# The later adaLN modulations of a two-layer mixer: vector times matrix by TensorE, or elementwise by VectorE with one-column products

## The chip, the cores and the metric

One core of one Trainium2 chip runs the whole program. The metric is the device time of one execution in microseconds; a kernel's time is the median over its runs.

## What is computed

Two layers over 1024 latent and 256 context tokens of width 1024. Each layer takes a modulated layer norm, one wide input projection, four token mixers, a gated merge of their outputs and an output projection. What the change touches is the modulation: for each of two conditions (`c` for the latent tokens, `c_ctx` for the context) a vector of 1024 numbers times a 1024 x 3072 matrix, plus a bias.

```python
def modulation(cond, w_mod, b_mod):
    mod = jax.nn.silu(cond) @ w_mod + b_mod
    return jnp.split(mod, 3, axis=-1)
...
    shift, scale, gate = modulation(c[:, None, :], w_mod, b_mod)
    p_lat = (layer_norm(x) * (1.0 + scale) + shift) @ w_in
    acc = sum(jax.nn.sigmoid(ms[i]) * ((ys[i] * jax.nn.silu(zs[i])) @ w_branch[i]) for i in range(N_BRANCH))
    x_new = layer_norm(DEEPNORM_ALPHA * x + gate * out) * ln_g + ln_b
```

## The kernel before

Most products take float32 operands split into a high and a low part (`hi_lo`, `split_w`), and each is done as three TensorE products (L299 to L301 and L307 to L309). The engines are TensorE (PE; its weight loads, the stationary operand, are listed as PEld), VectorE (DVE), ScalarE (ACT), GpSimd (POOL) and SyncE (SP), which issues most DMAs. The program is written as Python generators; `weave` takes steps from two of them in turn. A scheduler then sets a fixed order of the instructions on each engine, and each engine and each DMA queue works through its order without overtaking.

**The merge stage** (`merge`, L981 to L1004) follows the attention of each layer. For each of the four branches, in the order 2, 3, 1, 0, it loads the branch's output from DRAM (`load_u`: six loads `merge__tmp<-start__u`, L973, each split into `uh` and `ul` by ACT at L312 and DVE at L313). Then for each of eight column blocks `c` and each token group (256, 512 and 512 tokens in layer 0; 512 and 512 in layer 1) it makes a gate and a branch product. For even `c` the gate is computed there: 24 TensorE products into `merge__mm` (two PSUM buffers). For odd `c` the gate was computed during the attention and is loaded from DRAM (`merge__tmp<-start__gates`, L992). ACT takes the sigmoid (L996) into a `tmp` tile (three buffers). Six TensorE products into one of three banks of the PSUM tile `wide` give the branch product. DVE multiplies the two (L1000 for the first branch, L1002 after it) and adds (L1003, on POOL for odd `c`). Weights arrive as `merge__wraw` and are split by ACT (L263) and DVE (L264).

**The later modulations.** `modulation` for the first 2048 columns of layer 0 runs at the program's start. The others (`later_mods`: 1024 gate columns of layer 0, 2048 shift and scale columns of layer 1, 1024 gate columns of layer 1) are a generator that is woven into the merge stage of layer 0 as `mod0`. It loads 64 tiles of 128 rows x 512 columns of `w_mod` (`mod__wm`, tag `q`, three buffers, L185). The two condition vectors (`sc`, 128 x 2 for each of eight row blocks `k`) are the stationary operand, and 256 or 512 columns of weights stream past (L188): 96 float32 products into rows 0 and 1 of four column groups of one PSUM bank (tag `pv`, a single buffer). The result lies in rows, so ACT copies it out (L194, 12 copies), TensorE transposes it in 32 pieces of 128 columns (L197), and DVE adds the bias (L199). `last__gate` (L1014) then writes a gate to DRAM in 4-byte elements, and it is read back as rows in the output projection.

Of the kernel before, what the change touches and what calls it, by code (L numbers as in the profile page):

```python
# [8 lines left out]
F32 = mybir.dt.float32  # L9
F32R = mybir.dt.float32r  # L10
AF = mybir.ActivationFunctionType
ALU = mybir.AluOpType
# [5 lines left out]
KC = D // 128  # L18
# [29 lines left out]
def hybrid_kernel(ctx: ExitStack, tc, a):  # L48
    nc = tc.nc
    pe, act, dve, pool, sp = nc.tensor, nc.scalar, nc.vector, nc.gpsimd, nc.sync  # L50
# [3 lines left out]
    tp = ctx.enter_context(tc.tile_pool(name="tp", bufs=2))  # L54
    sm = ctx.enter_context(tc.tile_pool(name="sm", bufs=4))
    lc = ctx.enter_context(tc.tile_pool(name="lc", bufs=2))
# [19 lines left out]
    def nm(s):  # L76
        ids[0] += 1
        return f"{phase[0]}__{s}_{ids[0]}"
# [4 lines left out]
    def weave(*streams):  # L83

        live = [[0, n, label, gen] for label, gen, n in streams]
        while live:
            s = min(live, key=lambda s: (s[0] + 0.5) / s[1])
            phase[0] = s[2]
            s[0] += 1
            if next(s[3], live) is live:  # L90
                live.remove(s)
# [81 lines left out]
    def modulation(l, base, ncols, out, stage, sw):  # L173

        acc = ps_v.tile([128, 512], F32, tag="pv", name=nm("pm"))
        g = 4
        w_ = ncols // g
        n = ncols // 128
        bm = lc.tile([128, 16], F32, tag="bm", name=nm("bm"))
        sp.dma_start(bm[:, :n], a["b_mod"][l, :, base // 128:base // 128 + n])  # L180
        for k in range(KC):
            for h in range(ncols // sw):
                w = stage()
                c0 = base + h * sw
                sp.dma_start(w, a["w_mod"][l, k * 128:(k + 1) * 128, c0:c0 + sw])  # L185
                for j in range(sw // w_):
                    q = 32 * (h * sw // w_ + j)
                    pe.matmul(acc[q:q + 2, :w_], sc[:, k, :], w[:, j * w_:(j + 1) * w_],  # L188
                              start=k == 0, stop=k == KC - 1)
                yield  # L190
        tps = tbank()
        for j in range(g):
            row = tmp()
            act.copy(row[0:2, :w_], acc[32 * j:32 * j + 2, :w_])  # L194
            for i in range(w_ // 128):
                c = j * (w_ // 128) + i
                pe.transpose(tps[:, 2 * c:2 * c + 2], row[0:2, i * 128:(i + 1) * 128], ident[0:2, 0:2])  # L197
        mc = lc.tile([128, 2, 16], F32, tag="modc", name=nm("modc"), bufs=4)
        dve.tensor_tensor(mc[:, :, :n].rearrange("p s n -> p n s"),  # L199
                          tps[:, :2 * n].rearrange("p (n s) -> p n s", s=2),  # L200
                          bm[:, :n, None].to_broadcast([128, n, 2]), ALU.add)
        if n == 16:
            dve.tensor_scalar(mc[:, :, 8:16], mc[:, :, 8:16], 1.0, None, ALU.add)
        out["m"] = mc
        yield
# [109 lines left out]
    def layer(l, xh, xl, need_ctx, gate, finish, side, ahead=None):  # L315
# [663 lines left out]
        def merge():  # L979
            for bi, i in enumerate(M_ORDER):  # L980
                uh, ul = load_u(i, bi % 2 == 0)  # L981
                for c in range(KC):
                    w = None if (i, c) in gate_d else load_chunk(a["w_chunks"][l, GATE_0 + i * KC + c])
                    wb = load_chunk(a["w_branch"][l, i, c])
                    if bi == 0:
                        acc[c] = slot(s="acc")
                    for g in qgroups:
                        gs = slice(g[0], g[0] + g[1])
                        sgm = tmp()
                        if w is None:  # L990
                            pm = sgm
                            sp.dma_start(sgm[:, :g[1]], gate_d[i, c][:, gs])  # L992
                        else:
                            pm = mm()
                            mm_b(pm[:, :g[1]], w, xs_g(g))
                        act.activation(sgm[:, :g[1]], pm[:, :g[1]], AF.Sigmoid)  # L996
                        pb = sbank()
                        mm_b(pb[:, :g[1]], wb, lambda k: (uh[k][:, gs], ul[k][:, gs]))
                        if bi == 0:
                            dve.tensor_mul(acc[c][:, gs], pb[:, :g[1]], sgm[:, :g[1]])  # L1000
                        else:
                            dve.tensor_mul(sgm[:, :g[1]], pb[:, :g[1]], sgm[:, :g[1]])  # L1002
                            (pool if w is None else dve).tensor_add(acc[c][:, gs], acc[c][:, gs], sgm[:, :g[1]])  # L1003
                        yield  # L1004

        for _ in fill["gen"]:
            pass
        weave((f"merge{l}", merge(), 4 * KC * len(qgroups)), (f"mod{l}", side, 68))


        phase[0] = f"last{l}"
# [143 lines left out]
    ctx.push(pools)  # L1155
    x1 = dr.tile([SEQ, D], F32, name="x1", bufs=1)

    def raw_w():
        return tp.tile([128, 512], F32, tag="q", name=nm("wm"), bufs=3)

    def later_mods():
        yield from modulation(0, 2048, 1024, gate0, raw_w, 512)
        yield from modulation(1, 0, 2048, mc1, raw_w, 512)
        yield from modulation(1, 2048, 1024, gate1, raw_w, 512)

    def fin0(t, Y, later):
        if t >= CT:
# [99 lines left out]
```

## Time and profile before

| | |
|---|---|
| median of 3 runs | 2960.34 us (2957.03 to 2962.0) |
| the profiled execution | 2960.92 us, span 2959.1 us |
| busy in the span | PE 94%, DVE 51%, ACT 41%, POOL 14% |
| mean granted TensorE clock | 0.977 of full speed |
| chain of work that ended last | PE 75%, DVE 7%, DMA 4%, ACT 4% |

A busy share is an average over stages. A matmul's listed duration contains its latency; what it costs in a stream is the distance from its start to the start of the next. "Releaser" is the instruction that ended an engine's wait. For a DMA, the time "to landing" runs from its issue to the arrival of its data.

### The profile page before, as it was taken

What the parts mean: (1) busy time and instruction counts of PE and PEld (TensorE: products, weight loads), DVE (VectorE), ACT (ScalarE), POOL (GpSimd) and SP (SyncE); (2) the same over time, 40 slices, a digit from 0 to 9 for tenths busy, and PEclk for the clock granted to TensorE, in tenths of its full rate; (3) what the DMA queues carried; (4) which work ended last, traced back from release to release, by engine and by line L of the source; (5) the groups of instructions that cost most, each with busy time, mean ns of one, the idle gap of its engine ahead of it and who ended that gap; (6) DMA issues with size and microseconds to landing.
All of it is one profiled execution on the core that took longest, in us unless ns stands there. A gap on an engine that the chain in (4) does not pass through costs nothing.

```text
span 2959.1 us, 40218 instructions
## 1 busy us (share of the span) xinstructions
PE 2790.4 (94%) x14458; PEld 2253.0 (76%) x14458; DVE 1508.0 (51%) x3069; ACT 1219.0 (41%) x2631; POOL 418.8 (14%) x507
## 2 busy tenths in 40 slices
PE   7997979999999999899999798999999999999998
PEld 3785858888888887677767576778888888777776
DVE  5644266555555552232458554356555556533456
ACT  4344256445455542222234434346545455522230
POOL 1210020110111100111222120012111111001131
PEclk9998989999999999999999898999999999999999
DMA  6333322222223333333332333423222323222232
GB/s 248 115 107 102 107 72 84 84 84 87 88 88 123 103 98 111 104 120 104 124 98 90 91 103 111 117 74 102 80 93 78 106 103 126 87 94 87 86 109 91
DMA packets 240424, 301.83 MB, mean 102 GB/s; under 512 B 27488, under 2 KB 160096, under 8 KB 240224
## 3 DMA queue, kind: packets, MB, share of 16 engines
q1 hardware_dynamic: 134368, 225.58, 24.2%
q10 hardware_dynamic: 105856, 73.68, 8.0%
q8 instruction: 114, 1.87, 0.3%
q14 instruction: 86, 0.70, 0.1%
HBM read 217.11 MB, written 82.07 MB: 101 GB/s over the span
## 4 chain that ended last, share of the span: by engine, by line
PE 75%; DVE 7%; DMA 4%; ACT 4%; issue 2%; POOL 2%; ACTq 1%; SPq 0%; DVEq 0%; POOLq 0%
PE wide L639 6%; PE merge__mm L307 4%; PE merge__mm L308 4%; PE merge__mm L309 4%; PE wide L307 3%; PE wide L308 3%; PE wide L309 3%; PE m_att__t L584 3%; PE g_att__t L584 2%; PE a_att__mm L307 2%; PE a_att__mm L308 2%; PE a_att__mm L309 2%; PE m_att__mm L309 2%; PE m_att__mm L308 2%; PE m_att__mm L307 2%
## 5 line engine op out<-in xcount | busy, mean ns | idle before, releaser
L307 PE MATMUL merge__mm<-xh,merge__whi 128*128 128x512 f32 (+1 forms) x640 | 243.0, 380 | 0.9 <-ACT a_att__tmp L934 0.9
L308 PE MATMUL merge__mm<-xl,merge__whi 128*128 128x512 f32 (+1 forms) x640 | 239.6, 374 | 0.0
L309 PE MATMUL merge__mm<-xh,merge__wlo 128*128 128x512 f32 (+1 forms) x640 | 239.4, 374 | 0.0
L313 DVE TENSOR_TENSOR m_att__pl<-m_att__t,m_att__ph 128x384 fp32r<-128x384 f32 (+1 forms) x248 | 122.1, 508 | 117.2 <-ACT m_att__ph L312 78.8
L263 ACT CAST merge__whi<-merge__wraw 128x256 fp32r<-128x256 f32 (+1 forms) x128 | 65.6, 513 | 255.6 <-PE merge__mm L308 176.7
L1002 DVE TENSOR_TENSOR merge__tmp<-wide,merge__tmp 128x512 f32<-128x512 f32 (+1 forms) x120 | 76.5, 637 | 184.8 <-PE wide L309 161.2
L1003 POOL TENSOR_TENSOR merge__acc<-merge__acc,merge__tmp 128x512 f32<-128x512 f32 (+1 forms) x60 | 79.2, 1320 | 585.9 <-DVE merge__tmp L1002 585.8
L307 PEld LDWEIGHTS merge__mm<-xh,merge__whi 128*128 128x128 f32 x640 | 120.6, 188 | 44.5 <-issue 19.9
L312 ACT CAST m_att__ph<-m_att__t 128x384 fp32r<-128x384 f32 (+1 forms) x248 | 105.0, 439 | 115.3 <-PE m_att__t L584 103.5
L313 DVE TENSOR_TENSOR g_att__pl<-g_att__t,g_att__ph 128x384 fp32r<-128x384 f32 (+1 forms) x228 | 111.3, 514 | 79.6 <-ACT g_att__ph L312 58.4
L307 PE MATMUL wide<-merge__uh,merge__whi 128*128 128x256 f32 (+1 forms) x320 | 127.4, 398 | 20.4 <-ACT merge__uh L312 11.5
L264 DVE TENSOR_TENSOR merge__wlo<-merge__wraw,merge__whi 128x256 fp32r<-128x256 f32 (+1 forms) x128 | 71.0, 555 | 141.2 <-ACT merge__whi L263 134.3
L309 PEld LDWEIGHTS merge__mm<-xh,merge__wlo 128*128 128x128 f32 x640 | 120.8, 189 | 23.9 <-issue 0.4
L308 PEld LDWEIGHTS merge__mm<-xl,merge__whi 128*128 128x128 f32 x640 | 120.8, 189 | 22.3
L312 ACT CAST g_att__ph<-g_att__t 128x384 fp32r<-128x384 f32 (+1 forms) x228 | 97.7, 446 | 69.3 <-PE g_att__t L584 65.3
L307 PE MATMUL a_att__mm<-xh,a_att__whi 128*128 128x512 f32 (+1 forms) x320 | 123.8, 387 | 0.0
L641 DVE TENSOR_SCALAR_CACHE_REDUCE m_att__p<-wide 128x1280 f32<-128x1280 f32 (+1 forms) x72 | 98.7, 1371 | 42.1 <-PE wide L639 41.8
L309 PE MATMUL a_att__mm<-xh,a_att__wlo 128*128 128x512 f32 (+1 forms) x320 | 120.1, 377 | 0.0
L639 PE MATMUL wide<-g_att__ks,g_att__q 128*128 128x512 f32 (+1 forms) x400 | 103.5, 365 | 17.5 <-DVE g_att__p L641 16.3
L308 PE MATMUL a_att__mm<-xl,a_att__whi 128*128 128x512 f32 (+1 forms) x320 | 120.0, 375 | 0.0
L299 PE MATMUL a_proj__mm<-a_proj__whi,xh 128*128 128x256 f32 (+1 forms) x320 | 112.0, 351 | 8.1 <-ACT a_proj__tmp L809 4.5
L308 PE MATMUL wide<-merge__ul,merge__whi 128*128 128x256 f32 (+1 forms) x320 | 119.6, 374 | 0.0
(418 smaller groups left out, 7919.4 us busy)
## 6 DMA issues: line engine op xcount, KB each, us to landing
merge__wraw<-in_w_chunks_dram SPq DMA_DIRECT2D x64, 256.0 KB, 2.9
mod__wm<-in_w_mod_dram SPq DMA_DIRECT2D x64, 256.0 KB, 3.0
g_proj__wm<-in_w_mod_dram SPq DMA_DIRECT2D x16, 512.0 KB, 9.8
a_att__wraw<-in_w_chunks_dram SPq DMA_DIRECT2D x32, 256.0 KB, 2.7
merge__wraw<-in_w_branch_dram SPq DMA_DIRECT2D x64, 128.0 KB, 2.1
merge__tmp<-start__gates SPq DMA_DIRECT2D x32, 256.0 KB, 3.2
merge__tmp<-outp__gates SPq DMA_DIRECT2D x32, 256.0 KB, 3.4
g_att__wraw<-in_w_chunks_dram SPq DMA_DIRECT2D x28, 256.0 KB, 2.7
```

The lines of the kernel that those rows point to most:

```text
L264: (pool if by_pool else dve).tensor_sub(lo[:, :n], raw[:, :n], hi[:, :n])
L299: pe.matmul(ps, xh, wh[:, n0:n1], start=first and k == 0, stop=False)
L307: pe.matmul(ps, wh, xh, start=first and k == 0, stop=False)
L308: pe.matmul(ps, wh, xl, start=False, stop=False)
L309: pe.matmul(ps, wl, xh, start=False, stop=last and k == nk - 1)
L312: act.copy(hi, src)
L313: dve.tensor_sub(lo, src, hi)
L584: pe.transpose(tb[:, i * 128:(i + 1) * 128], pts[q0 + i][:, col:col + 128], ident)
L639: pe.matmul(wide[:, c0:c0 + w], qs[:, j, qi * 128:(qi + 1) * 128], k[:, c0:c0 + w], start=j == 0, stop=j == len(ks) - 1)
L641: dve.tensor_scalar(pt[:, :nk], wide[:, :nk], -scale, None, ALU.mult, ALU.min, accum_out=nb)
L1002: dve.tensor_mul(sgm[:, :g[1]], pb[:, :g[1]], sgm[:, :g[1]])
L1003: (pool if w is None else dve).tensor_add(acc[c][:, gs], acc[c][:, gs], sgm[:, :g[1]])
```

## The change

The three later modulations are computed in another way. A weight tile is multiplied by a per-partition scalar on DVE and added to one of two running sums (128 x 512, one for each condition; tags `ph` and `pl`, with three and two buffers, which the merge stage doesn't otherwise use). Eight row blocks go into each sum. Then 128 columns of a sum at a time are TensorE's stationary operand, and one column of -0.5 (`mhalf`) streams past, which sums over the 128 rows and leaves the result in a column already. DVE multiplies by -2 and adds the bias. The order of the loads is by 512 columns first, then by row block; their number and size stay. The number of steps told to `weave` goes from 68 to 76. The first modulation of layer 0 stays as it was.

```diff
+    def modulation_apart(l, base, ncols, out):
+
+        acc = ps_v.tile([128, 512], F32, tag="pv", name=nm("pm"))
+        n = ncols // 128
+        bm = lc.tile([128, 16], F32, tag="bm", name=nm("bm"))
+        sp.dma_start(bm[:, :n], a["b_mod"][l, :, base // 128:base // 128 + n])
+        for h in range(ncols // 512):
+            sums = [tp.tile([128, 512], F32, tag=tag, name=nm("ms"), bufs=b) for tag, b in (("ph", 3), ("pl", 2))]
+            for k in range(KC):
+                w = raw_w()
+                sp.dma_start(w, a["w_mod"][l, k * 128:(k + 1) * 128, base + h * 512:base + (h + 1) * 512])
+                for s in range(2):
+                    if k == 0:
+                        dve.tensor_scalar(sums[s], w, sc[:, k, s:s + 1], None, ALU.mult)
+                    else:
+                        dve.scalar_tensor_tensor(sums[s], w, sc[:, k, s:s + 1], sums[s], ALU.mult, ALU.add)
+                yield
+            for s in range(2):
+                for c in range(4):
+                    o = s * n + 4 * h + c
+                    pe.matmul(acc[:, o:o + 1], sums[s][:, c * 128:(c + 1) * 128], mhalf[:, 0:1], start=True, stop=True)
+            yield
+        mc = lc.tile([128, 2, 16], F32, tag="modc", name=nm("modc"), bufs=4)
+        dve.scalar_tensor_tensor(mc[:, :, :n], acc[:, :2 * n].rearrange("p (s n) -> p s n", s=2), -2.0,
+                                 bm[:, None, :n].to_broadcast([128, 2, n]), ALU.mult, ALU.add)
...
-        weave((f"merge{l}", merge(), 4 * KC * len(qgroups)), (f"mod{l}", side, 68))
+        weave((f"merge{l}", merge(), 4 * KC * len(qgroups)), (f"mod{l}", side, 76))
...
-        yield from modulation(0, 2048, 1024, gate0, raw_w, 512)
-        yield from modulation(1, 0, 2048, mc1, raw_w, 512)
-        yield from modulation(1, 2048, 1024, gate1, raw_w, 512)
+        yield from modulation_apart(0, 2048, 1024, gate0)
+        yield from modulation_apart(1, 0, 2048, mc1)
+        yield from modulation_apart(1, 2048, 1024, gate1)
```

Lines after the new function move down by 33 (L313 becomes L346, L1002 becomes L1035). The order of the instructions changes in and just before the merge stage of layer 0; in the rest of the program it stays.

**TensorE, between two column blocks of the merge.** The older order has five modulation products between the branch products of two blocks; a suffix `x2` stands for two alike:

```order
L307 MATMUL wide<-merge__uh_10946,merge__whi_10974 128x512
L308 MATMUL wide<-merge__ul_10947,merge__whi_10974 128x512
L309 MATMUL wide<-merge__uh_10946,merge__wlo_10975 128x512
L188 MATMUL mod__pm_11013<-mod__wm_11109,sc 2x256 x2
L188 MATMUL mod__pm_11013<-mod__wm_11123,sc 2x256 x2
L188 MATMUL mod__pm_11013<-mod__wm_11137,sc 2x256
L307 MATMUL wide<-merge__uh_10932,merge__whi_11094 128x256
```

In the newer order there are eight groups of eight one-column products, all between merge products (one group is cut in two); the second group:

```order
L342 MATMUL wide<-merge__uh_10946,merge__wlo_11520 128x512
L230 MATMUL mod__pm_11013<-mhalf,mod__ms_11321 128x1 x4
L230 MATMUL mod__pm_11013<-mhalf,mod__ms_11322 128x1 x4
L340 MATMUL merge__mm_11728<-xh,merge__whi_11711 128x256
```

Where 49 stretches of modulation products stood, nine stand now, and pieces of the next block's `merge__mm` products fill the places between branch products.

**VectorE, at the start of the merge stage.** Before (`ul` are the low parts of the branch's output, L1000 the first multiplications):

```order
L313 TENSOR_TENSOR merge__ul_10933<-merge__tmp_10934,merge__uh_10932 128x256
L313 TENSOR_TENSOR merge__ul_10933<-merge__tmp_10938,merge__uh_10932 128x512
L313 TENSOR_TENSOR merge__ul_10933<-merge__tmp_10942,merge__uh_10932 128x512
L313 TENSOR_TENSOR merge__ul_10947<-merge__tmp_10948,merge__uh_10946 128x256
L1000 TENSOR_TENSOR merge__acc_10978<-wide,merge__tmp_10979 128x256
```

Now, over the same stretch (`ms` are the running sums):

```order
L346 TENSOR_TENSOR merge__ul_10933<-merge__tmp_10938,merge__uh_10932 128x512
L225 SCALAR_TENSOR_TENSOR mod__ms_11321<-mod__wm_11452,sc,mod__ms_11321 128x512
L225 SCALAR_TENSOR_TENSOR mod__ms_11322<-mod__wm_11452,sc,mod__ms_11322 128x512
L225 SCALAR_TENSOR_TENSOR mod__ms_11321<-mod__wm_11473,sc,mod__ms_11321 128x512
L346 TENSOR_TENSOR merge__ul_10933<-merge__tmp_10942,merge__uh_10932 128x512
L346 TENSOR_TENSOR merge__ul_10947<-merge__tmp_10948,merge__uh_10946 128x256
L225 SCALAR_TENSOR_TENSOR mod__ms_11322<-mod__wm_11473,sc,mod__ms_11322 128x512
L225 SCALAR_TENSOR_TENSOR mod__ms_11321<-mod__wm_11487,sc,mod__ms_11321 128x512
L225 SCALAR_TENSOR_TENSOR mod__ms_11322<-mod__wm_11487,sc,mod__ms_11322 128x512
L1033 TENSOR_TENSOR merge__acc_10978<-wide,merge__tmp_10979 128x256
```

The steps of the merge keep their order, and the sums stand between them. Of the 128 sums 19 stand in DVE's order ahead of the first `ul`, and 32 more ahead of the last L1033 of the first branch's third column block (L1000 at 1134 us in the trace of before); the other 77 are spread over the rest of the stage.

**SyncE, at the second branch's start.** Before, both writes of layer 0's gate stand ahead of four of the six `start__u` loads:

```order
L973 DMA merge__tmp_11680<-start__u_26_128 128x256
L973 DMA merge__tmp_11684<-start__u_26_128 128x512
L180 DMA mod__bm_13147<-in_b_mod_dram 128x8
L1014 DMA last__gate_13919<-mod__modc_11666 128x8x1 x2
L278 DMA merge__wraw_12015<-in_w_branch_dram 128x256
L973 DMA merge__tmp_11688<-start__u_26_128 128x512
L973 DMA merge__tmp_11694<-start__u_26_128 128x256
L973 DMA merge__tmp_11698<-start__u_26_128 128x512
```

Now:

```order
L220 DMA mod__wm_12354<-in_w_mod_dram 128x512
L1006 DMA merge__tmp_11691<-start__u_26_128 128x512
L1006 DMA merge__tmp_11697<-start__u_26_128 128x256
L311 DMA merge__wraw_12031<-in_w_branch_dram 128x256
L1047 DMA last__gate_13972<-mod__modc_11669 128x8x1
L1006 DMA merge__tmp_11701<-start__u_26_128 128x512
L220 DMA mod__wm_12393<-in_w_mod_dram 128x512
L220 DMA mod__wm_12435<-in_w_mod_dram 128x512
L1006 DMA merge__tmp_11705<-start__u_26_128 128x512
L1047 DMA last__gate_13972<-mod__modc_11669 128x8x1
```

Four of the six loads of the branch's output stand ahead of the first gate write now, one stands between the two writes, and five loads of modulation weights stand among them (one before).

## Rows read from the trace of the kernel before

**Rows 1.** The page, busy time of each engine: us (share of the span) xinstructions.

```profile
PE 2790.4 (94%) x14458; PEld 2253.0 (76%) x14458; DVE 1508.0 (51%) x3069; ACT 1219.0 (41%) x2631; POOL 418.8 (14%) x507
```

**Rows 2.** Busy time by stretch: stretch, us, engines, granted clock, DMA share, GB/s.

```profile
1066.00:1092.00 26.00, 26.00 (x153) 22.24 (x152) 10.94 (x23) 7.66 (x18) 1.23 (x2) 1.00 0.34 109
1092.00:1134.00 42.00, 41.41 (x207) 30.79 (x210) 11.45 (x21) 11.50 (x22) 0.00 (x0) 1.00 0.39 126
1190.00:1200.00 10.00, 5.84 (x27) 3.76 (x25) 2.32 (x4) 1.93 (x4) 0.00 (x0) 1.00 0.65 47
1200.00:1210.00 10.00, 6.50 (x19) 4.48 (x19) 3.43 (x7) 3.00 (x6) 0.00 (x0) 0.66 0.38 112
1090.00:1505.00 415.00, 399.97 (x1971) 297.98 (x1971) 146.07 (x250) 111.89 (x238) 58.03 (x53) 0.99 0.38 116
2560.00:2900.00 340.00, 330.27 (x1381) 255.79 (x1380) 140.31 (x218) 99.97 (x194) 49.29 (x41) 0.99 0.31 98
```

**Rows 3.** Waits in 1090 to 1505 us: who waited for whom, us, times, longest.

```profile
PEld wide L307 <- DVE merge__tmp L1002: 12.6, 17, 1.7
PE wide L307 <- ACT merge__uh L312: 8.8, 3, 7.7
PEld wide L307 <- DVE merge__acc L1000: 1.3, 3, 0.4
PE mod__t L197 <- ACT mod__tmp L194: 1.1, 1, 1.1
```

**Rows 4.** PE's groups in 1090 to 1505 us: busy us, mean ns, idle before.

```profile
L188 PE MATMUL mod__pm<-mod__wm,sc 128*2 128x256 f32 (+1 forms) x192 | 41.2, 450 | 0.0
L197 PE MATMUL mod__t<-ident,mod__tmp 2*128 2x2 f32 x32 | 3.7, 204 | 1.1 <-ACT mod__tmp L194 1.1
```

**Rows 5.** PE's timeline: start us, duration us, what; columns of the moving operand before "f32".

```profile
1109.64 0.39 PE L308 MATMUL wide<-merge__ul,merge__whi 128*128 128x512 f32 x1
1109.86 0.39 PE L309 MATMUL wide<-merge__uh,merge__wlo 128*128 128x512 f32 x1
1110.18 1.03 PE L188 MATMUL mod__pm<-mod__wm,sc 128*2 128x256 f32 x10
1111.14 0.39 PE L307 MATMUL wide<-merge__uh,merge__whi 128*128 128x256 f32 x1
...
1485.27 0.60 PE L188 MATMUL mod__pm<-mod__wm,sc 128*2 128x256 f32 x4
1485.80 0.50 PE L307 MATMUL merge__mm<-xh,merge__whi 128*128 128x512 f32 x1
```

**Rows 6.** PE's timeline at transposes of 2 rows: two, then four in one stretch.

```profile
1185.31 0.28 PE L197 MATMUL mod__t<-ident,mod__tmp 2*128 2x2 f32 x2
1185.52 0.38 PE L309 MATMUL merge__mm<-xh,merge__wlo 128*128 128x256 f32 x1
...
1397.70 0.41 PE L197 MATMUL mod__t<-ident,mod__tmp 2*128 2x2 f32 x4
1398.04 0.39 PE L308 MATMUL merge__mm<-xl,merge__whi 128*128 128x256 f32 x1
```

**Rows 7.** PEld's timeline in the output projection: eight loads of 128 rows for transposes.

```profile
1560.73 1.03 PEld L238 LDWEIGHTS outp__t<-ident,outp__Y 128*128 128x128 f32 x8
1561.73 0.19 PEld L299 LDWEIGHTS wide<-last__whi,xh 128*128 128x128 f32 x1
```

**Rows 8.** Line L466 on DVE: ns least/median/most, starts, forms.

```profile
L466 DVE SCALAR_TENSOR_TENSOR a_att__y<-a_att__y,a_att__tmp x5: 426/691/692, 1078.5 to 2574.2; 128x512 f32<-128x512 f32 x4, 128x256 f32<-128x256 f32 x1
```

**Rows 9.** SP's timeline at the second branch's start.

```profile
1189.37 1.16 SPq L1014 DMA_DIRECT2D last__gate<-mod__modc  x2
1191.20 0.57 SPq L278 DMA_DIRECT2D merge__wraw<-in_w_branch_dram  x1
1191.89 1.69 SPq L973 DMA_DIRECT2D merge__tmp<-start__u  x3
```

**Rows 10.** The chain in 1085 to 1215 us: start us, us, what.

```profile
1191.89 10.60 DMA merge__tmp<-start__u
1202.52 0.93 ACT merge__uh L312 x2
1203.49 0.58 PE wide L307
```

**Rows 11.** The page, DMA issues: count, KB each, median us to landing.

```profile
mod__wm<-in_w_mod_dram SPq DMA_DIRECT2D x64, 256.0 KB, 3.0
```

**Rows 12.** DVE's timeline near the stage's end: one operation, started while POOL works and while not.

```profile
1483.20 1.24 DVE L264 TENSOR_TENSOR last__wboth<-last__wraw,last__wboth 128x512 fp32r<-128x512 f32 x1
...
1487.59 0.68 DVE L264 TENSOR_TENSOR last__wboth<-last__wraw,last__wboth 128x512 fp32r<-128x512 f32 x1
```

**Rows 13.** POOL's timeline over the first of them.

```profile
1482.90 3.89 POOL L1032 TENSOR_TENSOR xl<-merge__acc,xh 128x256 fp32r<-128x256 f32 x4 [0.51 <-ACT xh L1031]
```

More of the change, by code (lines that the diff above doesn't have):

```diff
@@ L201, in modulation, with raw_w @@
                           bm[:, :n, None].to_broadcast([128, n, 2]), ALU.add)
+        if n == 16:
+            dve.tensor_scalar(mc[:, :, 8:16], mc[:, :, 8:16], 1.0, None, ALU.add)
+        out["m"] = mc
+        yield
+    def raw_w():
+        return tp.tile([128, 512], F32, tag="q", name=nm("wm"), bufs=3)
+    def modulation_apart(l, base, ncols, out):
[18 more added lines that the diff above has]
+                    pe.matmul(acc[:, o:o + 1], sums[s][:, c * 128:(c + 1) * 128], mhalf[:, 0:1], start=True, stop=True)
+            yield
+        mc = lc.tile([128, 2, 16], F32, tag="modc", name=nm("modc"), bufs=4)
+        dve.scalar_tensor_tensor(mc[:, :, :n], acc[:, :2 * n].rearrange("p (s n) -> p s n", s=2), -2.0,
+                                 bm[:, None, :n].to_broadcast([128, 2, n]), ALU.mult, ALU.add)
         if n == 16:
@@ L1156, in hybrid_kernel @@
     x1 = dr.tile([SEQ, D], F32, name="x1", bufs=1)
-    def raw_w():
-        return tp.tile([128, 512], F32, tag="q", name=nm("wm"), bufs=3)
     def later_mods():
-        yield from modulation(0, 2048, 1024, gate0, raw_w, 512)
-        yield from modulation(1, 0, 2048, mc1, raw_w, 512)
-        yield from modulation(1, 2048, 1024, gate1, raw_w, 512)
+        yield from modulation_apart(0, 2048, 1024, gate0)
+        yield from modulation_apart(1, 0, 2048, mc1)
+        yield from modulation_apart(1, 2048, 1024, gate1)
     def fin0(t, Y, later):
```

## Prediction

> **What bounds the kernel now.** I read the busy times first: TensorE is busy for 94% of the span [rows 1]. An average hides stages with other limits, so I read next the stretch in which the changed work lies, 1090 to 1505 us, the merge of layer 0 [rows 2]. PE is busy there for 399.97 of 415 us, DVE for 146.07, ACT for 111.89 and POOL for 58.03. Time taken from PE is time taken from the stage, so long as nothing new makes PE wait; and PE idles for only 15.0 us. The waits say for what [rows 3]: once 7.7 us for `uh`, the branch's output at the start of the second branch, and otherwise waits of at most 1.7 us for DVE to read a bank of `wide`. The reader should see one more stretch in the same view: the merge of layer 1, 2560 to 2900 us, runs without any modulation beside it, and PE idles for 9.7 of 340 us [rows 2].
>
> **What goes.** The 96 float32 products leave 192 records and 41.2 us of busy PE [rows 4]. Durations overlap in a stream, so I go by the distance to the next start. Five products of 256 columns, ten records, hold PE from 1110.18 to 1111.14 us, 0.96 us; two hold it from 1485.27 to 1485.80, 0.53 us [rows 5]. There are 49 such stretches between 1092.6 and 1485.8 us, 21 of 0.52 or 0.53 us and 28 of 0.95 to 0.97 us, together 37.8 us. Each also starts late: the product ahead of it takes 0.32 us to the next start where the one before takes 0.22 [rows 5]. At 0.09 us for each of 49 that is 4.4 us more. The 32 transposes stand in 11 stretches of 0.21 us (two) to 0.34 us (four) [rows 6], together 2.9 us; with 1.0 us for their late starts and PE's wait of 1.1 us for ACT's copies [rows 3] that is 5.0 us. All of it lies on PE, the engine that sets the stage's length: **-47.2 us**. The 12 ACT copies count nothing: ACT is idle for 73% of the stage [rows 2].
>
> **What comes on PE.** Eight groups of eight one-column products. A float32 product has two weight loads and two passes (192 records for 96 products). With one column to stream the loads set the price: 128 loads of 128 columns. No row has that product. From below: four transposes in 0.34 us against two in 0.21 us [rows 6] give 0.06 us for each load of 128 columns from 2 rows with two columns streamed. From above: eight loads of 128 x 128, with 128 columns streamed behind each, take 1.0 us, 0.125 us each [rows 7]. I take the lower, since it is nearest in what streams: 128 x 0.06 = 7.7 us, and nine stretches with 0.17 us for late start and refill, 1.5 us: **+9.2 us**, at most 18. The Trainium skill (TensorE: Matmul & The Clock Gate, section on LDWEIGHTS) says that a weight load takes its columns divided by 1.2 per ns whatever the rows, an estimate of 107 ns here. By that the group of products would cost 15.2 us and the sum come out 6 us higher. Rows 6 are faster than this.
>
> **What comes on DVE.** 128 sums over 512 elements; L466 is such an operation on such operands, 0.69 us [rows 8], so 88 us. DVE's load in the stage goes from 146 to 234 us of some 380, 62%. It stays off the bound as an average. But the sums aren't spread evenly. 19 of them stand in what was 1066 to 1092 us: 10.9 + 19 x 0.69 = 24.0 us of work in 26. 32 stand in what was 1092 to 1134: 11.5 + 22.1 = 33.5 us in 42 [rows 2]. There DVE is nearly full. Every sum also delays the DVE operation behind it, and PE has 20 waits for DVE over a bank [rows 3]. If each grows by half a sum to a whole one, that is 7 to 14 us. I take **+10 us**; from below 0, if the order keeps every sum in a gap, from above 25, a sum's length for each of the 36 places where a DVE step on a loaded gate ends (three groups of four column blocks of three branches).
>
> **What moves.** Modulation products filled places where PE would have waited. Without them, at the idle share of layer 1's merge, 9.7 of 340, a stage of 377 us has 10.8 us of idle; this one has 15.0 less the one wait of 7.7. **+3.4 us**, from 0 to the same again. The 64 loads of modulation weights stay in number and bytes, use SP's queue as before and land in 3.0 us [rows 11]; they count nothing, while each finds one of three buffers free, by DVE's sums now and by PE before. Where that cover fails is the first rival.
>
> The wait of 7.7 us has a cause that the change moves. The two writes of the gate are issued at 1189.37, the next loads of the branch's output at 1191.89 [rows 9], and these land 10.6 us later [rows 10], with DMA at 65% busy and 47 GB/s [rows 2]. The granted clock is 0.66 in the 10 us after, part of them at the lower of its two levels, 1.2 instead of 2.4 GHz, after PE had waited; that costs 3.4 us. Now four of the six loads stand ahead of the first write and one between them, so that PE gets the 256 tokens' step and meets the missing data a step later. I take **-3 us**; from nothing to the whole 11 us.
>
> **The sum.** -47.2 + 9.2 + 10 + 3.4 - 3 = -27.6 us. The profiled execution took 2960.92 us, 0.6 us above the median of the runs; it becomes 2933.3. I forecast 2933 us. With the low ends it is 2960.9 - 47.2 + 9.2 - 11 = 2912, with the high ends 2960.9 - 47.2 + 18 + 25 + 6.8 = 2964.5.
>
> **The rivals.** *Slower: DVE late at the branch starts.* SP is in order. Among the loads of `start__u` at each of the four branch starts stand three to five loads of modulation weights, and each of these holds SP until two sums are done. If DVE lags behind its order there (it is 92% full ahead of the first start), a load holds SP for its predecessor's landing and two sums, 3.0 + 1.4 = 4.4 us. Three of them bring the last part 13 us late. The trace shows the price of 10.6 us: 7.7 us of idle PE and 3.4 us of clock; 13 us would cost about 13, and four starts 53. With this in place of the 10 us and the 3: 2960.9 - 47.2 + 9.2 + 3.4 + 53 = 2979 us. It decides where the loads together come over 3 us late, as PE has that much work queued (10.6 less 7.7). Against it: DVE has 15 idle us in 1066 to 1092 to take 13.1 us of sums.
>
> *Same: the adds on POOL.* An operation of DVE with two SBUF inputs took 1.24 us while POOL added and 0.68 while it didn't [rows 12, 13]. A sum is such an operation. If the 36 adds of loaded gates on POOL are each held by a sum, 0.69 us, and with them the `tmp` buffer into which the next gate is loaded, PE loses 25 us at its waits there beside my other terms: 2958 us, no difference to be told. The Trainium skill (SBUF — State Buffer, section Who interferes with whom) states it as a rule: an operation of DVE with two SBUF inputs and one of GpSimd that reads SBUF shut each other out for a whole instruction. Rows 12 and 13 agree, with 0.56 us of delay. Against it: POOL is busy for 58 of 415 us [rows 2], so few of the sums meet an add.
>
> *Faster still: the stall goes.* If all six loads land in time, the gain has 8 us more: 2925 us.
>
> *It doesn't do what it says:* the one-column products could cost as much as what goes, if each of the 128 loads and its drain stood alone, at some 0.3 us. Rows 6 and 7 speak against it; I give it 3%, within "same".
>
> **How the numbers follow.** Forecast 0.64, the stall gone 0.08, POOL 0.09, loads at their full price 0.03, DVE late 0.10; 0.06 for a forecast that loses most of its gain to waits that I don't see (2950 us). A measurement of this kernel tells 0.2%, 6 us, from no change. Faster: 0.64 + 0.08 + 0.06 and 0.02 of POOL's, 0.80. Same: the rest of POOL's and the loads at full price, 0.10. Slower: 0.10. The range runs from 2916, near the low ends, to 2958, POOL's case; it leaves out the slower side and little of the faster.
>
> **What would show it.** In the profile after: no L188 and no L197 from `mod`; L230 with 128 records and about 1.1 us for each group of eight; PE's busy time in the merge lower by 30 to 40 us; L223 and L225 together some 88 us on DVE at 0.69 us each; waits of PE for DVE over `wide` grown by about 10 us; one wait for `uh` shorter than 7.7 us. Wrong would be: waits of PE for `uh` at several branch starts, each with a clock below 1 behind it (the slower rival); L1036 on POOL with a mean above 1.7 us and PE's waits behind L1035 doubled (POOL); a group of one-column products of over 2.3 us.

## Result and profile after

| | before | after |
|---|---|---|
| median of the runs | 2958.69 us (4 runs) | 2926.77 us (4 runs) |
| ratio, 95% interval | | 0.9894, 0.9877 to 0.9911 |
| the profiled execution, span | 2959.1 us | 2925.0 us |
| PE busy in the span | 2790.4 us | 2762.2 us |

The change saves 31.9 us; 2933 us were forecast. The profile of after stands here in the order of the prediction's steps. First the page's busy times and the stretches that answer to [rows 1] and [rows 2] (stretch, us, then PE, PEld, DVE, ACT, POOL, granted clock, DMA share, GB/s):

```profile
PE 2762.2 (94%) x14362; PEld 2260.3 (77%) x14362; DVE 1591.5 (54%) x3197; ACT 1219.1 (42%) x2619; POOL 421.4 (14%) x507
```

```profile
1066.00:1090.00 24.00, 24.00 (x140) 20.48 (x139) 20.55 (x39) 6.51 (x15) 1.68 (x2) 1.00 0.44 131
1090.00:1132.00 42.00, 39.93 (x203) 32.87 (x201) 33.44 (x56) 12.87 (x25) 0.00 (x0) 1.00 0.63 200
1090.00:1473.00 383.00, 365.15 (x1848) 300.75 (x1847) 218.68 (x356) 108.24 (x224) 58.08 (x51) 0.99 0.42 123
1192.00:1202.00 10.00, 9.65 (x36) 7.42 (x37) 3.87 (x7) 1.90 (x4) 0.00 (x0) 0.84 0.57 92
1202.00:1212.00 10.00, 6.49 (x29) 5.24 (x28) 7.06 (x13) 3.40 (x7) 0.00 (x0) 0.83 0.69 137
2527.00:2867.00 340.00, 330.99 (x1382) 255.58 (x1381) 139.96 (x220) 100.31 (x193) 49.86 (x41) 0.99 0.31 98
```

The merge stage of layer 0 that took 1090 to 1505 us ends some 32 us earlier, and the merge of layer 1 comes 34 us earlier and is as it was (331.0 busy of 340 us, 330.3 before). PE idles for 17.85 us in the stage, 15.0 before. The busy time of DVE went from 146 to 219 us, and in the first 42 us it is 33.44 us, as worked out. PE works at a lower granted clock for 20 us behind 1192 us, 10 us at 0.66 before.

The waits in 1090 to 1473 us (who waited for whom: us, times, longest), to be read beside [rows 3]:

```profile
PEld wide L340 <- DVE merge__tmp L1035: 15.5, 25, 2.4
PE wide L340 <- DVE merge__tmp L1035: 8.8, 12, 1.9
PE wide L340 <- ACT merge__uh L345: 7.6, 5, 4.9
DVE mod__ms L225 <- DMA mod__wm<-in_w_mod_dram: 4.5, 7, 1.2
PE wide L340 <- DVE merge__acc L1033: 0.8, 2, 0.6
```

The wait of 7.7 us for `uh` is 4.9 us now; all of PE's waits for `uh` together went from 8.8 to 7.6 us. The waits of PE for DVE over `wide` are 9.6 us in 14 places. [Rows 3] shows those of its weight loads (PEld); PE's own, in the same view of before, are 5.1 us in 7:

```profile
PE wide L307 <- DVE merge__tmp L1002: 5.1, 7, 1.5
```

DVE hardly waits for weights, 4.5 us.

The longest of the waits for DVE belongs to the stall as well. SP's timeline at the second branch, to be read beside [rows 9]:

```profile
1184.40 0.43 SPq L1047 DMA_DIRECT2D last__gate<-mod__modc  x1
1185.68 0.33 SPq L1006 DMA_DIRECT2D merge__tmp<-start__u  x1
1186.35 1.65 SPq L220 DMA_DIRECT2D mod__wm<-in_w_mod_dram  x2
1188.27 0.33 SPq L1006 DMA_DIRECT2D merge__tmp<-start__u  x1
1188.65 0.43 SPq L1047 DMA_DIRECT2D last__gate<-mod__modc  x1
```

The wait of 4.9 us, which ends at 1192.35 us, is for the fourth of the six loads. It was issued at 1183.42 us, ahead of the first write, and still landed 8.4 us later, as ACT's timeline shows:

```profile
1191.89 0.41 ACT L345 CAST merge__uh<-merge__tmp 128x256 fp32r<-128x256 f32 x1 [5.38 <-DMA merge__tmp<-start__u]
```

The load issued at 1188.27 us lands 14.7 us later. ACT's, DVE's and PE's timelines then show a chain (start us, us, [idle before <-releaser]):

```profile
1203.00 0.62 ACT L345 CAST merge__uh<-merge__tmp 128x512 fp32r<-128x512 f32 x1 [5.17 <-DMA merge__tmp<-start__u]
```

```profile
1203.65 0.69 DVE L346 TENSOR_TENSOR merge__ul<-merge__tmp,merge__uh 128x512 fp32r<-128x512 f32 x1 [4.85 <-ACT merge__uh L345]
1204.26 0.68 DVE L1035 TENSOR_TENSOR merge__tmp<-wide,merge__tmp 128x512 f32<-128x512 f32 x1
```

```profile
1205.00 0.50 PE L340 MATMUL wide<-merge__uh,merge__whi 128*128 128x512 f32 x1 [1.94 <-DVE merge__tmp L1035]
```

DVE works in order: L346 waits 4.85 us for late data, L1035 stands behind it, and PE waits for the bank that L1035 is to read. No sum is in this chain. The next wait, 1.57 us at 1210.72 us, does have sums in it: ahead of its L1035 (at 1209.98 us) DVE waits for modulation weights and works on two sums.

```profile
1208.19 1.54 DVE L225 SCALAR_TENSOR_TENSOR mod__ms<-mod__wm,sc,mod__ms 128x512 f32<-128x512 f32 x2 [1.25 <-DMA mod__wm<-in_w_mod_dram]
```

The one-column products in PE's timeline (start us, duration us, what). What a group costs is the distance to the next start:

```profile
1098.26 0.40 PE L342 MATMUL merge__mm<-xh,merge__wlo 128*128 128x512 f32 x1
1098.49 1.84 PE L230 MATMUL mod__pm<-mhalf,mod__ms 128*128 128x1 f32 x16
1100.19 0.47 PE L340 MATMUL merge__mm<-xh,merge__whi 128*128 128x512 f32 x1
...
1174.43 1.84 PE L230 MATMUL mod__pm<-mhalf,mod__ms 128*128 128x1 f32 x16
1176.13 0.36 PE L340 MATMUL merge__mm<-xh,merge__whi 128*128 128x256 f32 x1
```

Sixteen loads and passes hold PE for 1.70 us, 0.106 us each; all 128 come to 13.5 us in nine stretches. They don't start late: the product ahead takes its usual 0.23 us. The Trainium skill (TensorE: Matmul & The Clock Gate, section on LDWEIGHTS) gives a load's time as its columns divided by 1.2 per ns, whatever the rows: an estimate of 107 ns for 128 columns. For these loads of 128 rows the trace agrees; for the loads of 2 rows in [rows 6], 0.06 us, it does not.

The loads of [rows 7] have 128 rows as well. On PE's own timeline in before, eight of those transposes hold PE for 0.79 us, 0.099 us each:

```profile
1560.96 1.04 PE L238 MATMUL outp__t<-ident,outp__Y 128*128 128x128 f32 x8
1561.75 0.48 PE L299 MATMUL wide<-last__whi,xh 128*128 128x512 f32 x1
```

The sums in DVE's lines (least/median/most ns):

```profile
L225 DVE SCALAR_TENSOR_TENSOR mod__ms<-mod__wm,sc,mod__ms x112: 735/746/1817, 1073.0 to 1392.9; 128x512 f32<-128x512 f32 x112
L223 DVE TENSOR_SCALAR mod__ms<-mod__wm,sc x16: 477/480/490, 1071.9 to 1374.6; 128x512 f32<-128x512 f32 x16
```

The groups of DVE's and POOL's work in the stage (busy us, mean ns) name the rest:

```profile
L225 DVE SCALAR_TENSOR_TENSOR mod__ms<-mod__wm,sc,mod__ms 128x512 f32<-128x512 f32 x98 | 78.1, 824 | 5.1 <-DMA mod__wm<-in_w_mod_dram 4.5
L1036 POOL TENSOR_TENSOR merge__acc<-merge__acc,merge__tmp 128x512 f32<-128x512 f32 (+1 forms) x35 | 44.0, 1257 | 313.3 <-DVE merge__tmp L1035 313.1
```

POOL's adds have a mean of 1.26 us, where they had 1.22 us before, so they are not held up as the rival of the adds on POOL had it. It is the sums that are: laid beside POOL's timeline, 13 of the 112 overlap an operation of POOL, and ten of these take 1.1 to 1.8 us; the other 99 have a mean of 0.75 us. No engine is shown to wait for a sum directly.

Where the 34.1 us between the two profiled spans lie can be read from PE's start times at three marks. From the first product of the merge (1089.50 before, 1087.47 after) to the first transpose of the output projection (1560.96 and 1529.72) the time is shorter by 29.2 us. Ahead of it lie 2.0 us, and in layer 1, up to its own merge (2573.85 and 2540.04), another 2.6 us, though the order of instructions is the same there. What that last piece comes from was not tried; in the traces of the other kernels that leave the gate's write in 4-byte elements it takes 1008.9 to 1012.3 us, against 1012.9 us before and 1010.3 us after.

### The profile page after: what moved, and what is told of

It is laid out like the page before. It is cut to its first block, busy times and chain, and to the rows that moved or that the text cites. A ratio compares the mean times of both kernels' runs of the same rounds, so it can differ in the third digit from the quotient of the medians.

```text
span 2925.0 us, 40154 instructions
## 1 busy us (share of the span) xinstructions
PE 2762.2 (94%) x14362; PEld 2260.3 (77%) x14362; DVE 1591.5 (54%) x3197; ACT 1219.1 (42%) x2619; POOL 421.4 (14%) x507
## 5 line engine op out<-in xcount | busy, mean ns | idle before, releaser
L346 DVE TENSOR_TENSOR m_att__pl<-m_att__t,m_att__ph 128x384 fp32r<-128x384 f32 (+1 forms) x248 | 122.1, 508 | 117.5 <-ACT m_att__ph L345 78.2
L346 DVE TENSOR_TENSOR g_att__pl<-g_att__t,g_att__ph 128x384 fp32r<-128x384 f32 (+1 forms) x228 | 111.3, 514 | 79.8 <-ACT g_att__ph L345 58.4
L1035 DVE TENSOR_TENSOR merge__tmp<-wide,merge__tmp 128x512 f32<-128x512 f32 (+1 forms) x120 | 76.3, 636 | 142.4 <-PE wide L342 135.2
L674 DVE TENSOR_SCALAR_CACHE_REDUCE g_att__p<-wide 128x1280 f32<-128x1280 f32 (+1 forms) x72 | 98.6, 1369 | 40.9 <-PE wide L672 32.7
```

Of the source, the lines that this page charges most:

```text
L346: dve.tensor_sub(lo, src, hi)
L674: dve.tensor_scalar(pt[:, :nk], wide[:, :nk], -scale, None, ALU.mult, ALU.min, accum_out=nb)
```

## Experiments

All ratios are to the kernel before, from runs on one chip beside it, with 95% intervals. One hundredth of the ratio is 29.6 us. The experiments ran on three chips, so two kernels are compared here by the difference of their ratios, which has an interval of some 5 to 7 us.

### What the one-column products cost

`no_products` takes them out of the kernel after; DVE copies elements of the sums in their place.

```diff
...
             for s in range(2):
-                for c in range(4):
-                    o = s * n + 4 * h + c
-                    pe.matmul(acc[:, o:o + 1], sums[s][:, c * 128:(c + 1) * 128], mhalf[:, 0:1], start=True, stop=True)
+                dve.tensor_copy(mc[:, s, 4 * h:4 * h + 4], sums[s].rearrange("p (c j) -> p c j", c=4)[:, :, 0])
...
```

> Leaves out the 64 one-column products; DVE copies one element of each sum in their place, so the modulation vectors are not the sums over rows. Theory A, the products cost what their weight loads take, 0.107 us each, and all of it lies on PE: 2926.8 - 13.5 = 2913 us, ratio to the kernel before 0.985. Theory B, the prediction's 9.2 us: 2917.6 us. Theory C, they fill places in which PE would wait for DVE anyway: no change, 2927 us, and PE's waits in the merge grow by as much as its busy time falls.

Measured: 2912.88 us, 0.9842 (0.9827 to 0.9856), 15 us less than after with an interval of some 7 us. Theory C, no change, falls: the products lie on PE's path. The figure is nearer to theory A's 13.5 us, but this run alone does not exclude theory B's 9.2 us. The order changed with the edit, too: the gate's first write is issued at 1117.8 us here, not at 1184.40, and PE's longest wait, 4.2 us, is in the first branch, while the second has none above a microsecond.

### What the gate's write costs, and through what

`gate_act` and `before_gate_act` send the four writes of `last__gate` through ACT's queue in place of SP's, one in the kernel after, one in the kernel before.

```diff
         for s in range(2):
-            sp.dma_start(gd[s].rearrange("(k p) -> p k", p=128), gate["m"][:, s, :KC])
+            act.dma_start(gd[s].rearrange("(k p) -> p k", p=128), gate["m"][:, s, :KC])
```

> The kernel after the change, with the four writes of the gate vector issued by ACT in place of SP. Theory A, the wait of 4.9 us for uh and the slow clock behind it come from the two gate writes that stand between the loads of the branch's output in SP's queue: both go, 2926.8 - 4.9 - 2 to 3 = 2919 to 2920 us. Rival 1, the small packets of the write take the DMA engines from whatever queue: no change, 2927 us, and the loads still take 10 us to land. Rival 2, the loads of modulation weights, held by DVE's sums, make them late: no change either, but the loads land within 4 us and are issued late.

> The kernel before the change, with the same four writes issued by ACT. Theory A: the wait of 7.7 us and the 3.4 us of slow clock go, 2959 - 11 = 2948 us. Rival (the writes hold the DMA engines from any queue): 2959 us, no change.

Measured: 2930.81 us, 0.9902 (0.9888 to 0.9915), against 0.9894 of after; and 2960.63 us, 1.0002 (0.9993 to 1.0011). Neither changes. Theory A, that the place in SP's queue is what costs, falls. PE's timeline of before_gate_act shows the same wait in the same place:

```profile
1202.66 0.58 PE L307 MATMUL wide<-merge__uh,merge__whi 128*128 128x256 f32 x1 [6.74 <-ACT merge__uh L312]
```

Its DMA queues in 1186 to 1206 us (packets, MB, share of the 16 engines' time) show the write by itself, since it now has a queue of its own, q10:

```profile
q1 hardware_dynamic: 1441, 1.97, 49.0%
q10 hardware_dynamic: 2080, 0.01, 32.3%
```

The two writes take 2080 packets for 0.01 MB and a third of all DMA engines' time over 20 us. Of the six loads of the branch's output beside them, issued by SP as ever, the median takes 6.2 us to land and the longest 11.2 us. In gate_act, in 1176 to 1196 us, the same packets have a smaller share:

```profile
q10 hardware_dynamic: 2080, 0.01, 12.0%
```

Loads beside them are as late all the same. A load of modulation weights issued at 1180.75 us lands after 11.2 us, the first two of the six loads take more than 10 us, and the other four are issued only from 1193.88 us on. Here DVE's sums do stand in the chain: they wait for the late weights, and L1033 behind them holds PE:

```profile
1192.00 1.42 DVE L225 SCALAR_TENSOR_TENSOR mod__ms<-mod__wm,sc,mod__ms 128x512 f32<-128x512 f32 x2 [7.83 <-DMA mod__wm<-in_w_mod_dram]
```

```profile
1194.50 0.55 PE L340 MATMUL wide<-merge__uh,merge__whi 128*128 128x256 f32 x1 [7.46 <-DVE merge__acc L1033]
```

So rival 1 holds for the first loads, and rival 2 (late issue behind the modulation weights) for the others. What in the packets holds the loads back is not settled: they have 32.3% of the engines' time in one trace and 12.0% in the other. The Trainium skill states two things that bear on it (DMA: Bandwidth & Descriptors): in its section on issuing engines, that DMAs from any engine run on the same 16 DMA engines and interleave; in its rules for kernel authors, that a last dimension that isn't contiguous becomes one descriptor for each element. The traces agree with the first, since the loads on SP's queue are late beside a write on ACT's, and with the second: two writes of 1024 elements, 2080 packets.

`after_rows` and `before_rows` turn the gate first, so that rows of 128 contiguous elements are written.

```diff
+        gps, row = tbank(), tmp()
+        for s in range(2):
+            pe.transpose(gps[:KC, s * 128:(s + 1) * 128], gate["m"][:, s, :KC], ident)
+        act.copy(row[:KC, :256], gps[:KC, :256])
         for s in range(2):
-            sp.dma_start(gd[s].rearrange("(k p) -> p k", p=128), gate["m"][:, s, :KC])
+            sp.dma_start(gd[s].rearrange("(k p) -> k p", p=128), row[:KC, s * 128:(s + 1) * 128])
```

> The kernel after the change, with the gate vector turned by two transposes on PE and one copy on ACT, so that its two writes have 8 packets of 512 bytes each instead of 1024 of 4 bytes. Theory A, the 4-byte packets hold the DMA engines for some 10 us from any queue, and the wait of 4.9 us for uh and the slow clock behind it come from that: 2926.8 - 4.9 - 2 to 3 = 2919 to 2920 us against the 2926.8 of after, no load of the branch's output over 5 us. Rival, the loads are issued late and would be late without the write: no change, 2927 us.

> The kernel before the change with the same turned gate vector. Theory A: the wait of 7.7 us and 3.4 us of slow clock go, 2959 - 11 = 2948 us. Rival: no change, 2959 us. In both, the difference of the two forms of the modulation stays: it was 34.2 us between the profiled runs less 2.8 us for the shorter wait, so after_rows should be some 29 to 31 us below before_rows.

Measured: 2916.85 us, 0.9853 (0.984 to 0.9867), 12 us below after; and 2953.38 us, 0.997 (0.9959 to 0.9981), 9 us below before. The rival, no change, falls in both. The two forms lie 34.6 us apart without the stall, with an interval of 5 us; 29 to 31 us were expected. The six loads of `start__u` at the second branch, from issue to landing, in after (the line's instructions in 1170 to 1200 us):

```profile
DMA to landing us min/median/max: 2.8/5.9/14.7
```

and in after_rows, for 1160 to 1195 us:

```profile
DMA to landing us min/median/max: 3.7/4.2/4.8
```

After_rows at the same place, PE's wait and its clock in the 20 us behind it:

```profile
1188.35 0.39 PE L340 MATMUL wide<-merge__uh,merge__whi 128*128 128x256 f32 x1 [1.29 <-ACT merge__uh L345]
```

```profile
1188.00:1198.00 10.00, 9.65 (x43) 7.92 (x44) 8.63 (x16) 3.69 (x8) 0.00 (x0) 1.00 0.49 156
1198.00:1208.00 10.00, 10.00 (x61) 8.58 (x60) 5.28 (x10) 3.15 (x7) 3.69 (x3) 1.00 0.36 109
```

The clock stays at its upper level where it was at 0.84 and 0.83 in after. PE's idle time in the merge goes from 17.85 us to 9.4 us:

```profile
1090.00:1468.00 378.00, 368.64 (x1879) 303.96 (x1877) 218.85 (x357) 110.90 (x230) 62.24 (x56) 1.00 0.40 125
```

One thing is mixed in: the turned write also comes later in the order, at 1457 us, and that of layer 1's gate at 2810 us (1477 us in after). The experiment shows the price of the 4-byte write where it stood, some 9 to 12 us; it does not tell the fewer packets from the other place.

### What the sums on DVE cost

`two_sums` leaves out 96 of the 128 sums.

```diff
                     if k == 0:
                         dve.tensor_scalar(sums[s], w, sc[:, k, s:s + 1], None, ALU.mult)
-                    else:
+                    elif k == KC - 1:
                         dve.scalar_tensor_tensor(sums[s], w, sc[:, k, s:s + 1], sums[s], ALU.mult, ALU.add)
```

> Leaves out 96 of the 128 sums on DVE (only the first and the last row block of each are summed); loads and one-column products stay. Theory A, DVE has room and its sums cost PE only some 4 us of waits over wide: 2922 to 2924 us. Theory B, the prediction's 10 us: 2917 us. Theory C, sums also hold the loads of modulation weights on SP and with them the loads of the branch's output: then the wait for uh at the second branch (4.9 us) goes too, 2915 us or less.

Measured: 2929.87 us, 0.9899 (0.9886 to 0.9913), no faster than after. None of the theories had that, and the run alone settles nothing. Its SP timeline has the gate's writes much earlier:

```profile
1111.18 0.43 SPq L1047 DMA_DIRECT2D last__gate<-mod__modc  x1
...
1129.56 0.43 SPq L1047 DMA_DIRECT2D last__gate<-mod__modc  x1
```

Its DMA issues of 1118.5 to 1123 us have a gate load (KB each, median us to landing) that took as long as the loads beside the write in before, [rows 10], and PE's timeline has two new waits, while that for `uh` at the second branch is gone:

```profile
merge__tmp<-start__gates SPq DMA_DIRECT2D x1, 256.0 KB, 10.0
```

```profile
1128.36 0.79 PE L340 MATMUL wide<-merge__uh,merge__whi 128*128 128x512 f32 x1 [5.83 <-DVE merge__acc L1033]
...
1153.07 0.58 PE L340 MATMUL wide<-merge__uh,merge__whi 128*128 128x256 f32 x1 [3.12 <-DVE merge__acc L1033]
```

The stall moved along with the first write (what the second wait of 3.12 us comes from was not followed up). So the sums were tried again without it. `two_sums_rows` is the same edit in after_rows; `sums_twice_rows` adds a second operation behind each accumulating sum:

```diff
                         dve.scalar_tensor_tensor(sums[s], w, sc[:, k, s:s + 1], sums[s], ALU.mult, ALU.add)
+                        dve.scalar_tensor_tensor(sums[s], w, 0.0, sums[s], ALU.mult, ALU.add)
```

> after_rows without 96 of the 128 sums on DVE (loads and one-column products stay), so that no gate write covers what the sums cost. Theory A, DVE has room: within 4 us of after_rows. Theory B, the prediction's +10 us for PE's waits behind DVE: 10 us below after_rows.

> after_rows with each of the 112 accumulating sums followed by another that adds zero, 112 x 0.78 = 87 us more on DVE, 330 of some 385 us busy. Theory A, DVE has room and orders its work by due time: up to 5 us above after_rows, 2917 to 2922 us. Theory B, each sum that is put ahead of a gate's product makes PE wait, as the prediction's +10 us had it: 10 us or more above after_rows, 2927 us or more.

Measured: 2918.75 us, 0.9856 (0.9843 to 0.987), the same as after_rows; and 2922.43 us, 0.9871 (0.9854 to 0.9887), 5 us above it, at the upper edge of theory A; the intervals of the two overlap. PE's largest wait for DVE over the merge, in before_rows:

```profile
PE wide L307 <- DVE merge__tmp L1002: 5.3, 6, 1.7
```

in after_rows:

```profile
PE wide L340 <- DVE merge__tmp L1035: 4.4, 10, 0.9
```

and in sums_twice_rows, with DVE's share behind it (295.65 of 383 us):

```profile
PE wide L341 <- DVE merge__tmp L1036: 9.6, 16, 1.8
```

```profile
1090.00:1473.00 383.00, 368.63 (x1877) 304.35 (x1876) 295.65 (x469) 110.63 (x230) 67.04 (x56) 1.00 0.41 125
```

There are more waits with the sums than before the change, and each is shorter; together they cost no more. Only with DVE at 77% do they grow, by 5 us, and PE's idle time in the merge grows from 9.4 to 14.4 us, which agrees with the difference of the times.

### The floor, and both forms against it

`no_mod_rows` is after_rows without the later modulations' loads, sums and products.

> after_rows without any of the later modulations' work: no loads of w_mod, no sums, no one-column products; the vectors are the bias alone. The floor of the stage. Theory A, products 13.5 us and nothing else on PE's path: 13 to 16 us below after_rows, 2901 to 2904 us; against before_rows 46 to 52 us, so that the old products cost the 47.2 us of the prediction. Theory B, sums and loads cost waits too: 23 us or more below after_rows.

Measured: 2903.0 us, 0.9803 (0.9786 to 0.982). After_rows lies 14.8 us above it (0.9853 less 0.9803), theory A: beside the products, the sums and loads cost nothing that shows. Before_rows lies 49.4 us above it: the old form's whole price, forecast as 47.2 us. Both figures have an interval of some 6 us.

The traces, one of each kernel, tell the same for the part of the program that the change touches. From the first product of the merge to the first transpose of the output projection, the marks used above:

| kernel | us |
|---|---|
| before | 471.5 |
| after | 442.3 |
| before_rows | 462.3 |
| after_rows | 431.0 |
| no_mod_rows | 417.8 |

By them the old form costs 44.5 us and the new one 13.2 us, 31.3 us apart, and the gate's write costs 9.2 us before and 11.2 us after the change.

### Fewer weight loads, and another order

`f32r_rows` rounds the last of the eight sums and multiplies in float32r, with two columns streamed; `f32r_rows_68` and `after_rows_68` also set the share of the side work back to 68.

```diff
+                        if k == KC - 1:
+                            rounded.append(tp.tile([128, 512], F32R, tag=("ph", "pl")[s], name=nm("mr"), bufs=3 - s))
...
-                    pe.matmul(acc[:, o:o + 1], sums[s][:, c * 128:(c + 1) * 128], mhalf[:, 0:1], start=True, stop=True)
+                    pe.matmul(acc[:, o:o + 2], rounded[s][:, c * 128:(c + 1) * 128], mhalf_r[:, 0:2], start=True, stop=True)
```

```diff
-        weave((f"merge{l}", merge(), 4 * KC * len(qgroups)), (f"mod{l}", side, 76))
+        weave((f"merge{l}", merge(), 4 * KC * len(qgroups)), (f"mod{l}", side, 68))
```

> after_rows with the last sum of each rounded to float32r and the products of two columns in float32r, one weight load and one pass each in place of two (64 loads instead of 128). Theory A, the loads set the price at 0.107 us each: 64 x 0.107 = 6.8 us below after_rows. Theory B, a product's price is its start, late by its own, whatever the loads: within 2 us of after_rows.

> after_rows with the side work's share in the weave at 68 as before the change, not 76, so that the same instructions come in a slightly different order. Theory A, the order within the merge decides only single waits of 1 to 2 us: within 4 us of after_rows. Theory B, the share of 76 is a part of what the change brings: over 6 us above after_rows.

> f32r_rows with the share at 68. Theory A, in f32r_rows the 7 us that the halved loads save on PE were given back by waits that came with that order: with another order 3 to 7 us below after_rows. Theory B, they are not to be had, because PE then waits for DVE instead: within 2 us of after_rows again.

Measured: f32r_rows 2916.64 us, 0.9848 (0.9835 to 0.9862); after_rows_68 2917.77 us, 0.9857 (0.984 to 0.9873); f32r_rows_68 2912.06 us, 0.9842 (0.9824 to 0.9859). PE's timeline of f32r_rows shows the price of a group halved:

```profile
1100.86 0.95 PE L235 MATMUL mod__pm<-mhalf,mod__mr 128*128 128x2 f32 x8
1101.67 0.47 PE L345 MATMUL merge__mm<-xh,merge__whi 128*128 128x512 f32 x1
```

Eight loads take 0.81 us, 0.101 us each: the price goes with the number of loads and passes, which is halved, not with that of products. The 7 us did not reach the end time of f32r_rows, 1.5 us below after_rows; that is theory B's figure, but not for its reason. Its order has a few longer waits, and a slower clock behind them, where after_rows has 1.00 in both stretches:

```profile
1247.00:1257.00 10.00, 9.55 (x42) 7.92 (x43) 3.22 (x7) 1.53 (x3) 3.69 (x3) 0.83 0.18 52
1450.00:1475.00 25.00, 21.37 (x90) 16.14 (x90) 9.70 (x15) 7.68 (x20) 10.86 (x13) 0.93 0.63 195
```

In the other order f32r_rows_68 lies 3.3 us below after_rows by the ratios, at the lower edge of theory A, and 4.4 us below after_rows_68. The intervals overlap, so that the gain is likely and not shown. After_rows_68 lies within 4 us of after_rows, as its theory A had it. The two orders of after_rows are both faster than before and after; f32r_rows_68 has the lowest median of the kernels that leave nothing out.

## Why the prediction was right, and which terms were not

The forecast was 2933 us from 2960.9, a gain of 27.6 us; the profiled execution took 2926.77 us, a gain of 34.1. Of that, 29.2 us lie between the merge's first product and the output projection, where all terms of the sum have their place; 4.6 us lie outside it, and no term is about them. The bound, PE, and the sign were right. By term, with the marks of the table above:

- **What goes, -47.2 us.** Right as far as can be told: 44.5 us by the marks, 49.4 us by the times of before_rows and no_mod_rows.
- **One-column products, +9.2 us.** Too low: 13.5 us in the trace, 13.2 by the marks and 14.8 by the times of after_rows and no_mod_rows, between the two bounds. The step that failed is the choice of the lower bound, "since it is nearest in what streams". The transposes of [rows 6] load 128 columns over 2 rows only, at 0.06 us, and a load over 128 rows took 0.106 us. The float32r products stream two columns as those transposes do, and still took 0.101 us for each load. No run varies the rows alone, so that the rows are the likely cause and not a shown one. [Rows 7], with 128 rows, was the nearer row, and PE's start times there give 0.099 us. The 1.5 us for late starts didn't come.
- **PE waits for DVE, +10, and idle as in layer 1's merge, +3.4 us.** Too high: before_rows and after_rows have 5.3 and 4.4 us of such waits over `wide`, and the new form's price is that of its products, so that the pair came to about nothing. "If each grows by half a sum to a whole one" was not borne out: taking 96 sums away gained nothing, and adding 112 cost some 5 us. The 20 waits that it counted are those of weight loads; PE's own were 7. In after the waits did grow, by 4.5 us, but 3.5 us of that are the two waits at 1205.00 and 1210.72 us in the wake of the gate's write, and only the second has sums in it.
- **The wait for `uh`, -3 us.** The wait fell by 2.8 us as said, but the stall's whole price didn't: the write costs 9 us in before and 11 to 12 in after, each with an uncertainty of several us. The reason given, its place among the loads in SP's order, was wrong. From ACT's queue the write cost the same; the fourth load, which stands ahead of both writes, took 8.4 us to land, and the last, between the two, 14.7 us, which brought a second wait.
- **The rivals.** No branch start but the second had a wait of more than a microsecond in after, so SP and DVE were not late there. The first rival's mechanism, DVE late behind modulation weights, shows at the second branch of gate_act, beside the write. POOL's adds kept a mean of 1.26 us; a group of products took 1.70 us, under the 2.3 us that would have cost the gain.

The high ends of the sum add up to 2963.5 us, not 2964.5; nothing rests on it.

That the forecast came within 6 us is in good part luck. By the marks three terms came out worse than worked out (what goes by 2.7 us, the products by 4.3, the gate's write by 5) and one better, PE's waits by 13.7 us. They nearly cancel, and leave 29.2 where 27.6 us were forecast.

## What to carry to other kernels

Where PE sets the end, work may go to an engine that has room in that stage. Here sums on DVE cost PE nothing that shows with DVE busy for 57% of the stage, and some 5 us at 77%. Count what comes back on PE by its weight loads, and price one by PE's start times at a load with as many rows. A few KB written in 4-byte elements are not a small transfer: look at the packets of a queue, not its bytes, and try turning such a vector on chip first. And compare two versions of a part with known stalls taken out of both, since two edits here (no_products and two_sums) moved the gate's write, and PE's waits with it.

## What had not been expected

- Two writes of 4 KB took 2080 packets, and 32% of 16 DMA engines over 20 us in one trace, 12% in another. Issued from either queue they cost the kernel the same, 9 to 12 us, through late loads and the clock behind PE's wait.
- A load issued 1 us ahead of such a write took 8.4 us to land.
- A weight load of 128 columns took 0.106 us over 128 rows and 0.06 us over 2 rows.
- DVE's busy time in the stage could double, from 146 of 415 us to 296 of 383 us, for some 5 us of PE's waits.
